# One two-bank PSUM tile kept for attention scores, single banks for every other matmul product

## The chip, the cores and the metric

The kernel runs on one core of a Trainium2 chip. The metric is the device time of one execution in microseconds (us). The kernel before took 1350.54 us (median of 3 runs, 1347.71 to 1353.4).

The core has five instruction streams that matter here: PE (the matrix engine, with its weight loads listed apart as PEld), DVE (vector), ACT (scalar), POOL (GpSimd) and SP, which issues the DMAs. Matmul results land in PSUM, which has 8 banks; one bank holds a 128 x 512 float32 block.

## The reference, cut to what matters

Two layers of a hybrid encoder over 512 tokens of width 1024. In each layer:

```python
h = rmsnorm(x)
proj = h @ w_in                      # group A: 8 q heads, 2 kv heads; group B: 4 heads with 2 q/k halves
# q and k: per-head RMSNorm, then rotary
ya = windowed_gqa_sink(qa, ka, va, sink)     # query blocks of 128, three neighbouring key blocks, mask
yb = diff_attention(qb, kb, vb, lam)         # softmax(first half) - lam * softmax(second half), all 512 keys
x = x + concat(ya, rmsnorm(yb)) @ w_out
h = rmsnorm(x)
gate, val = split(h @ w_up)                  # D_FF = 2816 = 22 blocks of 128
x = x + (silu(conv3(gate)) * val) @ w_down
```

Everything is float32. The kernel splits each operand into a high and a low part and forms each product from three matmuls (high x high, high x low, low x high), in `mm3` (L205).

## The kernel before

The residual stream `x` lies transposed in SBUF as 8 tiles of 128 x 512. Weights stream in as units of up to 512 KB. Each is copied to a high part by ACT (`wh`, L193) and its low part is formed by DVE or POOL (`wl`, L194); three such pairs of buffers exist, and `next_unit` prepares units up to three ahead.

A layer runs in these stages. `project` (L323) makes one 256-column chunk of the input projection for four token blocks, 24 matmuls a block; the first chunk is `akv`, then `aq0` and `aq1`, all run one after the other. Then `weave` (L133) interleaves two tracks by their written costs: `attend()` (L593), and a chain of the group-B projections (`proj_b`, L630) and the output projection (`out_pass`, `out_tail`). In `attend`, group A has 8 steps of `a_scores` and `a_values`, group B 16 steps of `b_scores`, `b_weights` and, for every second one, `b_values`. After the weave `out_last(1)` closes the output projection, the norm's factor `rb` is made (L686 to L692), and the feed-forward part (FFN) runs as two rounds: up-projection blocks `f` (12, then 10), then eight down-projection blocks `d`.

For each FFN block `f` there are two up products, gate and value, of 24 matmuls each. DVE multiplies the gate by `rb` (`gp`, L709), ACT, DVE and POOL do the convolution and the SiLU, DVE multiplies by the value product (L717), and `split_out` (L257) writes the result `act`. For each `d` a down product of 36 or 30 matmuls is added to `x` by DVE (L731).

PSUM before: tag `mm`, two single banks; tag `at`, two tiles of two banks each (`at2`, L94); `acc` and `tq`, one bank each. That is all eight banks.

- Scores take a two-bank `at` tile: `a_scores` two in turn for each step (L421), `b_scores` one for each step (L511).
- The transposed probabilities of group A, `pt`, take for key block 0 a two-bank `at` tile of which one half is used, for block 1 the `tq` bank, for block 2 an `mm` bank (L466). Those of group B, `wt`, take half of an `at` tile, and for the last head an `mm` bank (L540).
- `tq` also serves the transposes of q and k in `qk_out` (L366) and the two small products of `b_norm`. `mm` also serves `proj_b` and the output projection.
- `halves(both)` hands out the two halves of an `at` tile as two successive products (L390, L400). `halves(wide2)` does so for `out_last(1)` and the down products, and `wide2` for the two up products of a block: two times an `at` tile, every third time two `mm` banks.

The names in the profile show which it was: `up` and `dn` are halves of an `at` tile, `up_6a` or `dn_4b` is an `mm` bank.

The framework (Tile) assigns buffers and semaphores and orders the instructions of each engine when the kernel is built; on the chip each engine runs its list in that order.

Of the kernel before, what the change touches and what calls it, by code (L numbers as in the profile page):

```python
# [42 lines left out]
def kernel(  # L43
# [47 lines left out]
    def mm(name):  # L91
        return ps.tile([P, S], F32, tag="mm", bufs=2, name=name)

    def at2(name):  # L94
        return ps.tile([P, 2, S], F32, tag="at", bufs=2, name=name)

    def accum(name):
        return ps.tile([P, S], F32, tag="acc", bufs=1, name=name)
# [1 line left out]
    def tq(name):  # L100
        return ps.tile([P, S], F32, tag="tq", bufs=1, name=name)

    cyc = {"i": 0}

    def wide2(name):
        cyc["i"] += 1
        if cyc["i"] % 3 == 0:
            return mm(f"{name}a"), mm(f"{name}b")
        t = at2(name)
        return t[:, 0], t[:, 1]  # L110

    def halves(pick):
        have = []

        def alloc(name):
            if not have:
                have.extend(pick(name))
            return have.pop(0)
        return alloc

    def both(name):
        t = at2(name)
        return t[:, 0], t[:, 1]

    def run(gen):
        for _ in gen:
            pass
# [151 lines left out]
    for l in range(depth):  # L279
# [107 lines left out]
            split_out(va[0][:, t * P:(t + 1) * P], va[1][:, t * P:(t + 1) * P], raw[:, P:])  # L387
            qk_out(raw[:, :P], t, P, tabs[1], ka, "ka", None)

        run(project("akv", akv_done, halves(both)))  # L390
        rqa = sb.tile([P, NT, 4, 2], F32, tag="rqa", bufs=1, name=f"rqa{l}")
        rqb = sb.tile([P, NT, 4, 2], F32, tag="rqb", bufs=1, name=f"rqb{l}")
        qa = [(pair(f"qah{l}_{i}"), pair(f"qal{l}_{i}")) for i in range(2)]
# [3 lines left out]
                bank, t, CW, tabs[0], qa[i], f"qa{i}", rqa[:, t, 2 * i:2 * i + 2, :].rearrange("p a b -> p (a b)")), alloc)  # L397

        qk = {}
        pairs_at = halves(both)  # L400
        banks = iter((mm, mm, pairs_at, pairs_at, pairs_at, pairs_at, mm, mm))
        run(proj_a(0, lambda name: next(banks)(name)))
        run(proj_a(1, lambda name: next(banks)(name)))

        y_hi = [None] * 8
        y_lo = [None] * 8
# [5 lines left out]
        def a_scores(ip, qb):  # L412
            kb0, kb1 = max(qb - 1, 0), min(qb + 2, NT)
            n = (kb1 - kb0) * P
            m0 = (kb0 - qb + 1) * P
            nm = f"a{l}_{ip}_{qb}"
            q, k = qa[ip], ka
            mx = small(f"mx_{nm}", 4)
            so = []
            for i in range(2):  # L420
                sc = both(f"sc_{nm}_{i}")  # L421
                for j, (u, v) in enumerate(((0, 0), (0, 1), (1, 0))):
                    for g in range(2):
                        rs = slice(g * HD, (g + 1) * HD)
                        nc.tensor.matmul(sc[g][:, :n], lhsT=q[u][rs, i, qb * P:(qb + 1) * P],
                                         rhs=k[v][rs, kb0 * P:kb1 * P], start=j == 0, stop=j == 2)
                for g in range(2):
                    s = tmp(f"so_{nm}_{i}_{g}")
                    nc.vector.tensor_tensor_reduce(out=s[:, :n], in0=sc[g][:, :n], in1=mask_sb[:, m0:m0 + n],  # L429
                                                   op0=ALU.add, op1=ALU.max, scale=1.0, scalar=-3.0e38,  # L430
                                                   accum_out=mx[:, 2 * i + g:2 * i + g + 1])
                    so.append(s)
                yield 1.0
            by_g = lambda v: v.rearrange("p (g i) -> p i g", g=2)[:, 2 * ip:2 * ip + 2, :]
            pairs = lambda v: v.rearrange("p (i g) -> p i g", g=2)
            rq = rqa[:, qb, 2 * ip:2 * ip + 2, :]
            ngm = small(f"ng_{nm}", 4)
            nc.vector.tensor_tensor(out=pairs(mx), in0=pairs(mx), in1=rq, op=ALU.mult)
            nc.vector.scalar_tensor_tensor(out=pairs(ngm), in0=pairs(mx), scalar=-1.0, in1=by_g(nsink),
                                           op0=ALU.mult, op1=ALU.min)  # L440
            dn = small(f"dn_{nm}", 4)
            nc.vector.tensor_tensor(out=pairs(dn), in0=pairs(ngm), in1=by_g(sink), op=ALU.add)
            es = small(f"es_{nm}", 4)
# [12 lines left out]
            a_so[ip, qb] = so  # L456

        def a_values(ip, qb):
# [4 lines left out]
            pv = accum(f"pv_{nm}")  # L463
            pb = []
            for b in range(nkb):
                tr = mm(f"pt_{nm}_{b}") if b == 2 else both(f"pt_{nm}_{b}")[0] if b == 0 else tq(f"pt_{nm}_{b}")  # L466
                for g in range(2):
                    for i in range(2):
                        o = (2 * g + i) * P
                        nc.tensor.transpose(tr[:, o:o + P], so[2 * i + g][:, b * P:(b + 1) * P], ident)  # L470
                pt = prob(f"p_{nm}_{b}")
                split_out(pt[:, 0], pt[:, 1], tr)
                pb.append((pt[:, 0], pt[:, 1]))
                yield 0.5
# [25 lines left out]
        def b_scores(half, qb, j):  # L500
# [7 lines left out]
            rq = rqb[:, qb, h, :]  # L508
            q, k = qk[half]
            e = []  # L510
            sc2 = at2(f"sc_{nm}")  # L511
            sc = (sc2[:, 0], sc2[:, 1])
            for i, (u, v) in enumerate(((0, 0), (0, 1), (1, 0))):
                for c in range(2):
                    rs = slice(c * HD, (c + 1) * HD)
                    nc.tensor.matmul(sc[c], lhsT=q[u][rs, j, qb * P:(qb + 1) * P], rhs=k[v][rs, j, :],  # L516
                                     start=i == 0, stop=i == 2)
            nc.vector.tensor_reduce(out=mx, in_=sc2, axis=AX, op=ALU.max)
            nc.vector.scalar_tensor_tensor(out=mx, in0=mx, scalar=-1.0, in1=rq, op0=ALU.mult, op1=ALU.mult)  # L519
            for c in range(2):  # L520
                e.append(tmp(f"e_{nm}_{c}"))
# [11 lines left out]
        def b_weights(half, qb, j):  # L533
# [3 lines left out]
                b_st[half, j, "w"] = [prob(f"w{n}_b{l}_{h}_{qb}").rearrange("p a (b q) -> p (a b) q", b=2)  # L537
                                      for n in "hl"]
            wt = b_st[half, j, "w"]
            tr = (mm(f"wt_b{l}_{h}_{qb}") if half and j else both(f"wt_b{l}_{h}_{qb}")[0])  # L540
            for b in range(NT):
                nc.tensor.transpose(tr[:, b * P:(b + 1) * P], w[:, b * P:(b + 1) * P], ident)  # L542
            o = slice(qb % 2 * P, qb % 2 * P + P)
# [132 lines left out]
        def out_tail():  # L676
# [3 lines left out]

        weave((attend(), ATT),
              (chain(proj_b(0), proj_b(1), out_pass(0, mm), out_pass(1, mm), out_tail()), 98.6))
        run(out_last(1, w_last, halves(wide2)))
        norm.square(NK - 2)
        norm.square(NK - 1)
        r_tok2 = norm.rms()  # L686
# [11 lines left out]
        for pi, (f0, f1) in enumerate(FF_PARTS):  # L698
            act = []
            for f in range(f0, f1):  # L700
                acc = wide2(f"up{l}_{f}")
                for j in range(2):
                    w = next_unit()
                    for k in range(NK):
                        mm3(acc[j], (w[0][:, k, :], w[1][:, k, :]), (h.hi[k], h.lo[k]), k == 0, k == NK - 1)
                g = tmp(f"gp{l}_{f}", S + 2)
                nc.gpsimd.memset(g[:, 0:1], 0.0)
                nc.gpsimd.memset(g[:, S + 1:S + 2], 0.0)
# [10 lines left out]
                split_out(a[:, 0], a[:, 1], cv)  # L719
                act.append((a[:, 0], a[:, 1]))  # L720
            last = pi == len(FF_PARTS) - 1
            wide = halves(wide2)
            for d in range(NK):
                acc = wide(f"dn{l}_{pi}_{d}")
                nk = f1 - f0
# [85 lines left out]
```

## Time and profile before

| what | value |
|---|---|
| profiled execution, its own time | 1350.17 us |
| its span, first to last instruction | 1348.4 us |
| mean granted TensorE clock | 0.967 |
| runs | 1347.71, 1350.54, 1353.4 us |
| busy: DVE / ACT / POOL | 759.9 / 550.7 / 382.9 us |
| first layer: projections, attention, output projection | about 0 to 315 us |
| first layer: FFN | about 315 to 690 us |
| second layer: the same two parts | about 690 to 975 us, 975 to 1348 us |

How to read the lines below. A row of grouped instructions has line, engine, operation, what is written and read, shape and count, then busy time and the mean of one in ns, then the idle time of the engine just before them and what ended it. A row of waits has the waiting engine and line, what it waited for, and then total us, times, longest. A row of the timeline has start and duration in us; an idle time of the engine before the instruction stands in square brackets with what ended it. PE's matmuls are pipelined, so a matmul of 512 columns is listed with about 0.39 us while the next one starts about 0.23 us after it. A row of the chain of waits has start, length and the work that the end of the program hung on at that moment. A row of the windows has, for each engine, busy us and number of instructions in that stretch, then the granted clock.

### The profile page before, as it was taken

Reading aid. Unit: us, or ns where it says so; the run is one execution under the profiler, and the core shown is the slowest. Engines: PE = TensorE matmul, PEld = TensorE weight load, DVE = VectorE, ACT = ScalarE, POOL = GpSimd, SP = SyncE. Lnnn points to the kernel's source line nnn. Section 1 sums busy time; section 2 is a strip of 40 time slices with the busy share of each in tenths; the row PEclk is TensorE's granted clock in tenths of the full one; section 3 lists DMA queues with packets and bytes.
Section 4 is the critical chain, followed back from the end, with each engine's and each line's share of the span. In section 5 each row is a group of like instructions: output and inputs, shape, how many; then the busy total and the mean of one; then the engine's idle time right before and its main releaser. Section 6 shows DMA issues by size and latency. Waiting matters only on the chain.

```text
span 1348.4 us, 17285 instructions
## 1 busy us (share of the span) xinstructions
PE 1256.2 (93%) x6648; PEld 1048.1 (78%) x6648; DVE 759.9 (56%) x1345; ACT 550.7 (41%) x1003; POOL 382.9 (28%) x438
## 2 busy tenths in 40 slices
PE   6988799899999999999999688989999999999998
PEld 5977687687888778887788576967888887788876
DVE  6657687667555324554357676757755543355432
ACT  4445565445433212333345455634544331233321
POOL 5855377123211000110147461742221110011100
PEclk7998899699999999999999989989999999999999
DMA  4211122012332233332322020111133222333232
GB/s 167 82 44 32 40 63 63 16 47 79 95 101 90 82 101 94 98 100 69 98 91 63 32 63 8 57 63 32 48 99 104 94 87 90 106 94 97 83 102 78
DMA packets 32625, 102.93 MB, mean 76 GB/s; under 512 B 3616, under 2 KB 4000, under 8 KB 32544
## 3 DMA queue, kind: packets, MB, share of 16 engines
q1 hardware_dynamic: 32544, 101.84, 24.3%
q8 instruction: 52, 0.85, 0.3%
q14 instruction: 29, 0.24, 0.1%
HBM read 99.73 MB, written 2.10 MB: 76 GB/s over the span
## 4 chain that ended last, share of the span: by engine, by line
PE 75%; DVE 12%; ACT 5%; issue 4%; POOL 3%; DMA 1%; SPq 0%; POOLq 0%; ACTq 0%; DVEq 0%
PE up L207 8%; PE up L208 8%; PE up L206 8%; PE dn L207 4%; PE dn L206 4%; PE dn L208 4%; ACT so_a L447 2%; DVE so_a L454 2%; PE wo L206 1%; PE wo L207 1%; PE wo L208 1%; PE sc_b L516 1%; DVE so_a L429 1%; ACT wh L193 1%; PE wt_b L542 1%
## 5 line engine op out<-in xcount | busy, mean ns | idle before, releaser
L193 ACT CAST wh<-wr 128x1024 fp32r<-128x1024 f32 (+3 forms) x210 | 197.6, 945 | 401.4 <-PE up L207 151.7
L194 DVE TENSOR_TENSOR wl<-wr,wh 128x1024 fp32r<-128x1024 f32 (+3 forms) x174 | 191.7, 1105 | 170.0 <-ACT wh L193 165.0
L716 POOL TENSOR_TENSOR cv<-cv,rb 128x512 f32<-128x512 f32 x44 | 57.0, 1297 | 536.5 <-ACT cv L715 536.5
L207 PE MATMUL up<-nf_l,wh 128*128 128x512 f32 x464 | 180.9, 390 | 1.0 <-DVE nf_l L225 1.0
L206 PE MATMUL up<-nf_h,wh 128*128 128x512 f32 x464 | 180.6, 389 | 0.0
L208 PE MATMUL up<-nf_h,wl 128*128 128x512 f32 x464 | 180.5, 389 | 0.0
L194 POOL TENSOR_TENSOR wl<-wr,wh 128x1024 fp32r<-128x1024 f32 x36 | 86.7, 2413 | 99.4 <-ACT wh L193 85.7
L207 PEld LDWEIGHTS up<-nf_l,wh 128*128 128x128 f32 x464 | 87.1, 188 | 19.7 <-DVE nf_l L225 1.9
L206 PE MATMUL dn<-act,wh 128*128 128x512 f32 x240 | 96.1, 400 | 6.4 <-ACT wh L193 3.5
L206 PEld LDWEIGHTS up<-nf_h,wh 128*128 128x128 f32 x464 | 87.1, 188 | 18.1
L208 PEld LDWEIGHTS up<-nf_h,wl 128*128 128x128 f32 x464 | 87.1, 188 | 17.8
L207 PE MATMUL dn<-act,wh 128*128 128x512 f32 x240 | 95.9, 400 | 0.4 <-DVE act L259 0.4
L208 PE MATMUL dn<-act,wl 128*128 128x512 f32 x240 | 94.9, 398 | 0.0
L522 ACT ACTIVATE e_b<-sc_b,mx_b,rqb 128x512 f32<-128x512 f32 x64 | 49.3, 775 | 49.0 <-DVE mx_b L519 42.2
L709 DVE TENSOR_TENSOR gp<-up,rb 128x512 f32<-128x512 f32 x29 | 20.1, 692 | 80.6 <-PE up L208 79.6
L206 PEld LDWEIGHTS dn<-act,wh 128*128 128x128 f32 x240 | 45.4, 189 | 20.9 <-ACT wh L193 4.3
L715 ACT ACTIVATE cv<-cv 128x512 f32<-128x512 f32 x44 | 27.6, 632 | 79.7 <-DVE cv L714 79.6
L207 PEld LDWEIGHTS dn<-act,wh 128*128 128x128 f32 x240 | 45.8, 191 | 11.9 <-DVE act L259 1.1
L208 PEld LDWEIGHTS dn<-act,wl 128*128 128x128 f32 x240 | 45.4, 189 | 10.6
L206 PE MATMUL pj_bv<-wh,na_h 128*128 128x256 f32 x128 | 41.0, 320 | 7.7 <-DVE vb L376 7.7
L731 DVE TENSOR_TENSOR x<-x,dn 128x512 f32<-128x512 f32 x22 | 15.1, 688 | 52.8 <-PE dn L208 52.8
L470 PE MATMUL pt_a<-ident,so_a 128*128 128x128 f32 x160 | 28.3, 293 | 17.3 <-DVE so_a L454 12.0
(506 smaller groups left out, 3268.6 us busy)
## 6 DMA issues: line engine op xcount, KB each, us to landing
wr<-w_up SPq DMA_DIRECT2D x88, 512.0 KB, 3.6
wr<-w_in SPq DMA_DIRECT2D x36, 512.0 KB, 3.5
wr<-w_down SPq DMA_DIRECT2D x32, 384.0 KB, 3.1
wr<-w_down SPq DMA_DIRECT2D x32, 320.0 KB, 2.9
wr<-w_out SPq DMA_DIRECT2D x16, 512.0 KB, 3.7
x<-xT SPq DMA_DIRECT2D x8, 256.0 KB, 5.7
outT<-x SPq DMA_DIRECT2D x8, 256.0 KB, 2.0
rows<-row_par SPq DMA_DIRECT2D x2, 260.0 KB, 4.2
```

The costliest lines, as they stand in the source:

```text
L193: nc.scalar.copy(hi[:, o], raw[:, o])
L194: eng.tensor_tensor(out=lo[:, o], in0=raw[:, o], in1=hi[:, o], op=ALU.subtract)
L206: nc.tensor.matmul(acc, lhsT=a[0], rhs=b[0], start=start, stop=False)
L207: nc.tensor.matmul(acc, lhsT=a[0], rhs=b[1], start=False, stop=False)
L208: nc.tensor.matmul(acc, lhsT=a[1], rhs=b[0], start=False, stop=stop)
L447: nc.scalar.activation(so[i][:, :n], so[i][:, :n], AF.Exp, bias=ngm[:, i:i + 1], scale=rqa[:, qb, 2 * ip + i // 2, i % 2:i % 2 + 1], accum ...
L454: nc.vector.tensor_scalar(out=so[i][:, :n], in0=so[i][:, :n], scalar1=rl[:, i:i + 1], scalar2=None, op0=ALU.mult)
L470: nc.tensor.transpose(tr[:, o:o + P], so[2 * i + g][:, b * P:(b + 1) * P], ident)
L522: nc.scalar.activation(e[c], sc[c], AF.Exp, bias=mx[:, c:c + 1], scale=rq[:, c:c + 1], accum_out=lsum[:, c:c + 1])
L709: nc.vector.tensor_tensor(out=g[:, 1:S + 1], in0=acc[0], in1=rb, op=ALU.mult)
L715: nc.scalar.activation(cv, cv, AF.Silu)
L716: nc.gpsimd.tensor_tensor(out=cv, in0=cv, in1=rb, op=ALU.mult)
```

## The change

Tag `at` becomes two single banks, and a new tag `sc` holds one two-bank tile. PSUM is again full: `mm` 2, `at` 2, `sc` 2, `acc` 1, `tq` 1.

- Scores of both groups take the one `sc` tile.
- `pt` takes the two `at` banks in turn, for all key blocks; `wt` takes an `at` bank, and as before an `mm` bank for the last head.
- `akv`, `aq0`, `aq1` take `mm` and `at` banks in turn (`turn`).
- `out_last(1)`, the up products and the down products take `mm`, `at`, `mm`, `at` and one half of `sc` in a round of five (`wide`). Each up product now has a tile of its own.

No instruction is added or removed; what changes is where products land, and with it buffers, waits and the order that the framework makes.

```diff
-    def at2(name):
-        return ps.tile([P, 2, S], F32, tag="at", bufs=2, name=name)
+    def at(name):
+        return ps.tile([P, S], F32, tag="at", bufs=2, name=name)
+
+    def sc2(name):
+        return ps.tile([P, 2, S], F32, tag="sc", bufs=1, name=name)
...
-    def wide2(name):
+    def wide(name):
         cyc["i"] += 1
-        if cyc["i"] % 3 == 0:
-            return mm(f"{name}a"), mm(f"{name}b")
-        t = at2(name)
-        return t[:, 0], t[:, 1]
-
-    def halves(pick):
...
-    def both(name):
-        t = at2(name)
-        return t[:, 0], t[:, 1]
+        i = cyc["i"] % 5
+        return sc2(name)[:, 0] if i == 4 else (mm, at)[i % 2](name)
+
+    def turn(name):
+        cyc["i"] += 1
+        return (mm, at)[cyc["i"] % 2](name)
...
-        run(project("akv", akv_done, halves(both)))
+        run(project("akv", akv_done, turn))
...
-        pairs_at = halves(both)
-        banks = iter((mm, mm, pairs_at, pairs_at, pairs_at, pairs_at, mm, mm))
-        run(proj_a(0, lambda name: next(banks)(name)))
-        run(proj_a(1, lambda name: next(banks)(name)))
+        run(proj_a(0, turn))
+        run(proj_a(1, turn))
...
-                sc = both(f"sc_{nm}_{i}")
+                scp = sc2(f"sc_{nm}_{i}")
+                sc = (scp[:, 0], scp[:, 1])
...
-                tr = mm(f"pt_{nm}_{b}") if b == 2 else both(f"pt_{nm}_{b}")[0] if b == 0 else tq(f"pt_{nm}_{b}")
+                tr = at(f"pt_{nm}_{b}")
...
-            sc2 = at2(f"sc_{nm}")
-            sc = (sc2[:, 0], sc2[:, 1])
+            scp = sc2(f"sc_{nm}")
+            sc = (scp[:, 0], scp[:, 1])
...
-            tr = (mm(f"wt_b{l}_{h}_{qb}") if half and j else both(f"wt_b{l}_{h}_{qb}")[0])
+            tr = (mm if half and j else at)(f"wt_b{l}_{h}_{qb}")
...
-        run(out_last(1, w_last, halves(wide2)))
+        run(out_last(1, w_last, wide))
...
             for f in range(f0, f1):
-                acc = wide2(f"up{l}_{f}")
+                acc = []
                 for j in range(2):
                     w = next_unit()
+                    a = wide(f"up{l}_{f}_{j}")
                     for k in range(NK):
-                        mm3(acc[j], (w[0][:, k, :], w[1][:, k, :]), (h.hi[k], h.lo[k]), k == 0, k == NK - 1)
+                        mm3(a, (w[0][:, k, :], w[1][:, k, :]), (h.hi[k], h.lo[k]), k == 0, k == NK - 1)
+                    acc.append(a)
...
-            wide = halves(wide2)
             for d in range(NK):
                 acc = wide(f"dn{l}_{pi}_{d}")
```

More of the change, by code (lines that the diff above doesn't have):

```diff
@@ L103 @@
     cyc = {"i": 0}
-    def wide2(name):
+    def wide(name):
         cyc["i"] += 1
-        if cyc["i"] % 3 == 0:
-            return mm(f"{name}a"), mm(f"{name}b")
-        t = at2(name)
-        return t[:, 0], t[:, 1]
-    def halves(pick):
[L113 to L119, printed above, removed]
-    def both(name):
-        t = at2(name)
-        return t[:, 0], t[:, 1]
+        i = cyc["i"] % 5
[3 more added lines that the diff above has]
+        return (mm, at)[cyc["i"] % 2](name)
     def run(gen):
@@ L517, in b_scores @@
                                      start=i == 0, stop=i == 2)
-            nc.vector.tensor_reduce(out=mx, in_=sc2, axis=AX, op=ALU.max)
+            nc.vector.tensor_reduce(out=mx, in_=scp, axis=AX, op=ALU.max)
             nc.vector.scalar_tensor_tensor(out=mx, in0=mx, scalar=-1.0, in1=rq, op0=ALU.mult, op1=ALU.mult)
```

## The prediction

> **What bounds the kernel now.** I read the page first, then the windows by stage, then the chain of waits and PE's own waits in the stages that have gaps.
>
> ```profile
> span 1348.4 us, 17285 instructions
> PE 1256.2 (93%) x6648; PEld 1048.1 (78%) x6648; DVE 759.9 (56%) x1345; ACT 550.7 (41%) x1003; POOL 382.9 (28%) x438
> PE 75%; DVE 12%; ACT 5%; issue 4%; POOL 3%; DMA 1%; SPq 0%; POOLq 0%; ACTq 0%; DVEq 0%
> ```
>
> PE is busy for 93% of the span, and three quarters of the chain that ends last is PE. The rest is PE waiting. Where it waits, the windows tell (us of the stretch, then busy us and count of PE, PEld, DVE, ACT, POOL, then the granted clock):
>
> ```profile
> 60.00:180.00 120.00, 100.35 (x685) 86.67 (x684) 83.80 (x228) 64.21 (x165) 59.63 (x57) 0.91 0.15 47
> 235.00:300.00 65.00, 56.99 (x306) 45.39 (x307) 41.75 (x77) 27.84 (x56) 10.62 (x6) 0.84 0.10 30
> 315.00:443.00 128.00, 128.00 (x572) 106.22 (x573) 69.03 (x82) 47.07 (x59) 20.54 (x41) 1.00 0.31 95
> 443.00:507.00 64.00, 61.51 (x260) 48.30 (x259) 22.72 (x27) 14.83 (x18) 1.37 (x3) 1.00 0.30 91
> ```
>
> In the up-projection (315 to 443) PE never stops. In the down-projection (443 to 507) it does, with every other engine under half busy. In group A's attention (60 to 180) and in the end of group B's (235 to 300) it stops more, and the granted clock falls to 0.91 and 0.84. The change touches all four places in a different way, so I cost them apart.
>
> **Down products: the wait inside a shared tile.** Chain of waits near the end of the first layer (start, length, what):
>
> ```profile
> 674.41 0.02 issue
> 674.43 0.70 DVE x L731
> 675.26 0.47 PE dn L206
> ```
>
> One down product ends, DVE adds it to `x`, and only then does PE begin the next. The two are the halves of one `at` tile, in different banks: the framework keeps the second half's first matmul behind the read of the first half. Where it can, it slips a later product in:
>
> ```profile
> 645.00 0.39 PE L208 MATMUL dn<-act,wl 128*128 128x512 f32 x1
> 646.02 0.50 PE L206 MATMUL dn_4a<-act,wh 128*128 128x512 f32 x1 [0.63 <-ACT wh L193]
> ```
>
> Here the halves were those of `d` 2 and 3. PE turned to `d` 4, whose weights were not copied yet, so the wait is named ACT, but its origin is the same. All waits of this kind (total us, times, longest):
>
> ```profile
> PE dn L206 <- ACT wh L193: 3.5, 5, 0.9
> PE dn_2a L206 <- ACT wh L193: 1.4, 2, 0.7
> PE dn L206 <- DVE x L731: 1.7, 2, 0.9
> PE dn_6a L206 <- ACT wh L193: 0.7, 1, 0.7
> PE dn_4a L206 <- ACT wh L193: 0.6, 1, 0.6
> ```
>
> That is 11 waits, 7.9 us. The rotation of `wide2` gives 16 pairs of down products, of which 5 lie in `mm` (`dn_2a`, `dn_4a`, `dn_0a`, `dn_6a` and once more `dn_2a`) and 11 in `at`: one wait for each `at` pair and none for an `mm` pair. A listed idle time begins at the modelled end of a matmul, 0.39 us after its start, while matmuls otherwise follow at 0.23, so each wait loses 0.16 more: 7.9 + 11 x 0.16 = 9.7 us. With single banks each pair becomes like `mm`'s, and nothing of this lies beside other PE work. What is late next: the weights of the next `d`, which the `mm` pairs have in time. I take all 9.7; the bounds are 1.7 + 2 x 0.16 = 2.0 (only the waits named DVE) and 9.7.
>
> **Up products: the gate waits for its value.** DVE's timeline:
>
> ```profile
> 1027.40 0.69 DVE L709 TENSOR_TENSOR gp<-up,rb 128x512 f32<-128x512 f32 x1 [3.31 <-PE up L208]
> 1038.28 0.69 DVE L709 TENSOR_TENSOR gp<-up,rb 128x512 f32<-128x512 f32 x1 [2.71 <-PE up L208]
> 1043.72 0.69 DVE L709 TENSOR_TENSOR gp<-up_6a,rb 128x512 f32<-128x512 f32 x1 [1.86 <-PE up_6a L208]
> ```
>
> Two blocks in `at` are 10.88 us apart, two products of 5.44; the block after them, in `mm`, has its gate only 5.44 later. So an `at` gate waits until the value product too is done. That costs nothing while PE has more up products, but at the end of a round the down products need the last `act`. Second layer, second round, chain of waits and then PE's timeline:
>
> ```profile
> 1287.82 0.70 DVE cv L717
> 1288.54 0.63 ACT act L258
> 1289.19 0.70 DVE act L259
> 1292.51 0.43 PE dn L206
> ...
> 1289.21 0.50 PE L206 MATMUL dn<-act,wh 128*128 128x512 f32 x1 [1.19 <-ACT act L258]
> 1289.93 0.50 PE L207 MATMUL dn<-act,wh 128*128 128x512 f32 x1 [0.23 <-DVE act L259]
> ```
>
> The two waits lose 1.19 + 0.23 + 2 x 0.16 = 1.7 us, and afterwards some 8 matmuls run at 0.43 instead of 0.23, another 1.6 (the row at 1292.51 is one of them). With the gate 5.44 us earlier, `act` is ready about that much earlier, or at worst 2.0 us (0.70 + 0.63 + 0.70) after the last value product; both are in time. Gain 3.3, between 0 (if ACT's weight copies then stand in the way) and 3.3. The FFN together: 9.7 + 3.3 = 13.0 us.
>
> **FFN, five banks for six.** In steady state a bank comes round after 5 x 5.44 = 27 us and is held for its 5.44 and the few us until DVE has read it; down products are longer still. The tight place is the head of the second layer's FFN, where `rb` comes late and nothing is released meanwhile:
>
> ```profile
> 1004.42 0.69 DVE L717 TENSOR_TENSOR cv<-cv,up_0b 128x512 f32<-128x512 f32 x1 [2.09 <-POOL cv L716]
> 1005.44 0.39 PE L206 MATMUL up_3a<-nf_h,wh 128*128 128x512 f32 x1
> ```
>
> The seventh product begins at 1005.44. In a round of five it takes the second one's bank, free at 1005.11. Slack 0.3 us: I take 0, bounds 0 and 2 (a `rb` two us later, in one layer).
> The Trainium skill's page "Perfetto Trace Analysis", section "Matmul Optimizations", wants all eight PSUM banks in use, and here six in rotation become five. By that rule the FFN would slow down; the rows above have room for it in one place only.
>
> **Attention, what goes.** Scores, `pt`, `wt`, q/k transposes and projections no longer share banks, but for the last head. PE's waits for another product's bank:
>
> ```profile
> PE pt_a L470 <- DVE bql L259: 5.3, 2, 3.8
> PE sc_b L516 <- DVE p_a L259: 2.2, 2, 1.9
> PE sc_b L516 <- DVE wl_b L259: 1.2, 3, 0.6
> PE sc_a L425 <- DVE p_a L259: 1.1, 1, 1.1
> ```
>
> Together 9.8 us over both layers (the first is `pt` behind a q transpose in `tq`). PE works in a fixed order, so a wait that goes may uncover one for data just behind it; I take 6, bounds 0 and 9.8, the lower where every wait has another behind it.
>
> **Attention, what comes.** One score tile in place of two. The lengths, by groups and from the chain of waits, and last the window of the tail for `sc_b` alone (DVE's 8 maxima are 8 steps):
>
> ```profile
> L429 DVE CUSTOM_DVE_ANT_0 so_a<-sc_a,mask_sb 128x384 f32<-128x384 f32 x32 | 16.1, 552 | 7.6 <-PE pt_a L470 7.6
> L518 DVE TENSOR_REDUCE mx_b<-sc_b 128x2 f32<-128x1024 f32 x32 | 38.9, 1216 | 4.6 <-PE sc_b L516 4.6
> L259 DVE TENSOR_TENSOR p_a<-pt_a,p_a 128x512 fp32r<-128x512 f32 x40 | 26.7, 683 | 0.5 <-ACT p_a L258 0.2
> L258 ACT CAST p_a<-pt_a 128x512 fp32r<-128x512 f32 x40 | 22.4, 584 | 23.1 <-PE pt_a L470 22.9
> ...
> 122.45 0.73 PE sc_a L425 x6
> 183.21 0.89 PE sc_b L516 x6
> 239.22 1.64 ACT e_b L522 x4
> ...
> 235.00:300.00 65.00, 10.16 (x48) 5.14 (x48) 9.74 (x8) 13.03 (x32) 0.84 0.10 30
> ```
>
> Group A: the second tile's six matmuls (0.73) now wait for both masked maxima of the first (2 x 0.55), and DVE for them: at most 16 steps x 0.73 = 11.7. Queued behind PE's wait are projections, `pv` products and transposes, and ACT's exponentials wait for the maxima. But a step takes 120 / 8 = 15 us and its two scores in a row 2 x (0.73 + 1.10) = 3.7, so the order has room: I take 4. Third `pt` block: two `at` banks for three blocks, so it waits for the first block's copy and difference, 0.58 + 0.68 = 1.27, in the 40 - 2 x 16 = 8 steps that have three: at most 10.2; I take 2, since PE has projections to go on with. Group B: the next scores wait for the exponentials (1.64) instead of running beside them, at most 0.89 for each of the 32 steps, 28; but a step alone takes 0.89 + 1.22 + 1.64 = 3.75 against 65 / 8 = 8.1 us in the tail and `proj_b` fills PE before it, so only steps that follow closely pay: I take 3. Behind that wait stand `wt` transposes and output products, and L518 waits for the scores. Sum 9, bounds 0 (a wait more gains nothing by itself) and 50; I stay near the low end because PE's row 60 to 180 has work of its own for 100 of 120 us.
>
> `akv`, `aq0`, `aq1` over single banks: no price, PE is held by the matmuls themselves. No DMA moves, and no queue is passed.
>
> **Sum.** Against the profiled execution's 1350.2 (span 1348.4 and 1.8 around it, 0.4 under the median): 1350.2 - 13.0 - 6 + 9 = 1340.2, so 1340.
>
> **Rivals.** Single scores decide (slower): in both groups the score chain becomes the longest one, each of the 16 A steps pays 0.73, each third block 1.27, and the 16 steps of the two tails 0.89 and half as much again at a lower clock: 11.7 + 10.2 + 21 = 43, less 6 and 13: 1374 at full price. From 26 us of attention cost on it is slower by over 0.5%. For it: the chain of waits runs through L447, L454 and L518 where PE has gaps. Against it: 3.7 of 15 us.
> The page "TensorE: Matmul & The Clock Gate", section "Part 1: The HAM clock gate", has the clock halve after an idle window of about 3.4 us, and by it a tail with more waits would lose more than their sum. The rows agree in part: 0.84 in the tail, and 0.43 for 0.23 after 1289.93, though no single wait there was that long.
>
> Attention gains too: the removed bank waits come back whole and the new ones hide: 1350.2 - 13.0 - 9.8 = 1327, or some us less if the clock of 0.91 recovers. For it: in the 120 us of A no engine but PE is over 70% busy.
>
> Nearly no change: either the waits named ACT are truly late weights, and only 2.0 of the 9.7 goes (1350.2 - 2.0 - 3.3 + 3 = 1348), or attention loses about what the FFN gains.
>
> Five banks are too few: `rb` is later in the new order and the FFN's head stalls in both layers, 2 each: 1344, at the border of the same.
>
> **Numbers.** Forecast 0.42 (1332 to 1344), attention gains too 0.20, nearly no change 0.18, five banks 0.05, scores decide 0.15. 0.5% is 6.7 us, about what a measurement of this kernel can tell: faster means below 1343.8. Faster 0.42 + 0.20 = 0.62, same 0.18 + 0.05 = 0.23, slower 0.15. The range takes in 1327 with a little clock, and goes up past the same: 1322 to 1358.
>
> **What would show it.** Right: no wait of a `dn` product for ACT `wh` or DVE `x` in the middle of a down-projection, about 3 us less in each of the first layer's two; `gp` 5.44 us apart throughout; no wait of `pt` for `bql`. Wrong: `dn` waits that stay; waits of `sc_a` for L429 or of `sc_b` for L522 that sum to over 10 us; a stretch from 60 to 300 that has grown by more than 10.

## The result, and the profile after

The changed kernel takes 1303.74 us (median of 4 runs, 1300.81 to 1304.01), beside 1350.68 for the kernel before on the same chip: ratio 0.9648, 95% interval 0.9623 to 0.9673, faster. A second set of 5 runs gave 1302.88 us, 0.9635 (0.9616 to 0.9655). The forecast was 1340 with a range of 1322 to 1358, so the result lies 18 us below the range. The profiled execution took 1303.46 us.

The page of the kernel after, its span and busy times:

```profile
span 1301.2 us, 17328 instructions
PE 1242.6 (95%) x6648; PEld 1040.4 (80%) x6648; DVE 763.8 (59%) x1345; ACT 551.7 (42%) x1003; POOL 383.7 (29%) x438
```

The engines do the same work: the counts of all five are those of the kernel before, and the 43 instructions that the first row has more are of kinds that are not counted as busy. The span is 47.2 us shorter. In the new numbering a line is 7 to 9 lower: `mm3` is L198 to L200, `split_out` L250 and L251, the scores L416 and L507, `pt` L461, the gate `gp` L702.

Four stages divide the span but for some 4 us at its end, each measured between the starts of its first and last matmuls (us; the two layers with a slash):

| stage | before | after | difference |
|---|---|---|---|
| start, or last `dn`, to first `sc_a` (projections `akv`, `aq`) | 60.6 / 37.9 | 55.6 / 36.6 | -6.2 |
| first `sc_a` to last `wo` (attention, output projection) | 249.2 / 250.4 | 236.5 / 236.9 | -26.2 |
| last `wo` to first `dn`, and the up products of the second round | 242.73 / 241.97 | 242.45 / 242.45 | +0.2 |
| four rounds of down products | 261.01 | 246.55 | -14.5 |

The down rounds first, by the windows (stretch, then PE, PEld, DVE, ACT, POOL busy with counts, granted clock, DMA). The kernel before, its four rounds:

```profile
443.48:514.20 70.72, 68.23 (x288) 53.74 (x287) 24.16 (x28) 15.88 (x19) 1.37 (x3) 1.00 0.31 92
623.30:682.10 58.80, 56.67 (x240) 44.74 (x239) 24.76 (x32) 21.51 (x31) 9.06 (x7) 1.00 0.32 94
1103.40:1172.50 69.10, 67.71 (x289) 53.87 (x288) 24.01 (x28) 15.87 (x19) 1.37 (x3) 1.00 0.32 94
1281.50:1343.80 62.30, 58.80 (x241) 45.87 (x239) 19.31 (x26) 12.18 (x17) 1.34 (x1) 0.97 0.30 93
```

The kernel after:

```profile
425.50:492.80 67.30, 67.30 (x289) 54.10 (x288) 21.61 (x25) 14.43 (x17) 0.11 (x3) 1.00 0.33 96
601.80:657.80 56.00, 56.00 (x240) 45.02 (x239) 24.72 (x32) 21.55 (x31) 8.35 (x7) 1.00 0.34 99
1064.80:1132.10 67.30, 67.30 (x289) 54.10 (x288) 21.61 (x25) 14.41 (x17) 0.08 (x3) 1.00 0.33 96
1241.10:1297.10 56.00, 56.00 (x241) 45.01 (x239) 17.08 (x23) 10.83 (x15) 0.03 (x1) 1.00 0.33 104
```

PE is now busy for the whole of each stretch, and the list of PE's waits has none for a `dn` or `up` product. The end of the second layer's second round, DVE's timeline after:

```profile
1235.84 0.69 DVE L702 TENSOR_TENSOR gp<-up,rb 128x512 f32<-128x512 f32 x1 [3.09 <-PE up L200]
...
1241.35 0.69 DVE L710 TENSOR_TENSOR cv<-cv,up 128x512 f32<-128x512 f32 x1 [2.33 <-PE up L200]
```

The last gate is read 5.5 us before the last value product, one product earlier than a shared tile allowed. PE goes from the last up product (1240.86) to the first down product (1241.08) without a wait.

Attention with the output projection, first layer, by the windows, before and then after:

```profile
60.60:309.80 249.20, 220.00 (x1426) 187.32 (x1426) 177.66 (x402) 129.32 (x298) 117.05 (x109) 0.92 0.15 46
```
```profile
55.60:292.10 236.50, 215.75 (x1424) 182.61 (x1424) 169.96 (x401) 126.05 (x293) 116.00 (x108) 0.94 0.15 46
```

Nearly the same matmuls, 29.2 us of idle PE before and 20.8 after, at a higher clock. Group A alone, in the first layer after (its counterpart, 60 to 180, stood at a clock of 0.91):

```profile
55.00:160.00 105.00, 97.33 (x714) 85.61 (x715) 79.57 (x227) 64.37 (x166) 59.26 (x58) 0.98 0.18 54
```

PE's longest waits after (what it waited for, total us, times, longest):

```profile
PE sc_b L507 <- ACT e_b L513: 10.7, 8, 3.3
PE wt_b L533 <- DVE e_b L521: 8.6, 5, 3.4
...
PE tr_bk L361 <- DVE bkl L251: 4.9, 3, 2.7
PE pj_bq L198 <- ACT raw_bq L335: 4.0, 2, 2.0
PE pt_a L461 <- DVE so_a L445: 3.1, 2, 2.2
PE sc_a L416 <- DVE mx_a L420: 2.8, 5, 1.1
```

The single score tile does cost something: group B's scores now wait 10.7 us for the exponentials of the step before. It is outweighed. No wait of `pt` for `bql` is left, and nothing in this list is as large as the gain. In both layers together idle PE in this stage fell from 62.4 to 42.6 us, and PE was busy for 430.8 us with the same matmuls in place of 437.2.

### The profile page after: what moved, and what is told of

It reads as the page before. It is cut to its first block, busy times and chain, and to the rows that moved or that the text cites. A ratio compares the mean times of both kernels' runs of the same rounds, so it can differ in the third digit from the quotient of the medians.

```text
span 1301.2 us, 17328 instructions
## 1 busy us (share of the span) xinstructions
PE 1242.6 (95%) x6648; PEld 1040.4 (80%) x6648; DVE 763.8 (59%) x1345; ACT 551.7 (42%) x1003; POOL 383.7 (29%) x438
## 5 line engine op out<-in xcount | busy, mean ns | idle before, releaser
L199 PE MATMUL up<-nf_l,wh 128*128 128x512 f32 x704 | 274.9, 391 | 0.3
L198 PE MATMUL up<-nf_h,wh 128*128 128x512 f32 x704 | 274.0, 390 | 0.0
L200 PE MATMUL up<-nf_h,wl 128*128 128x512 f32 x704 | 273.5, 390 | 0.5
L199 PEld LDWEIGHTS up<-nf_l,wh 128*128 128x128 f32 x704 | 132.1, 188 | 30.4 <-DVE nf_l L217 3.5
L200 PEld LDWEIGHTS up<-nf_h,wl 128*128 128x128 f32 x704 | 132.2, 188 | 28.9 <-DVE wl L186 2.0
L198 PEld LDWEIGHTS up<-nf_h,wh 128*128 128x128 f32 x704 | 132.1, 188 | 27.6 <-ACT nf_h L216 0.5
L200 PE MATMUL dn<-act,wl 128*128 128x512 f32 x352 | 139.5, 397 | 0.0
L199 PE MATMUL dn<-act,wh 128*128 128x512 f32 x352 | 139.4, 397 | 0.0
L198 PE MATMUL dn<-act,wh 128*128 128x512 f32 x352 | 138.8, 395 | 0.0
L702 DVE TENSOR_TENSOR gp<-up,rb 128x512 f32<-128x512 f32 x44 | 30.3, 692 | 101.4 <-PE up L200 96.3
L199 PEld LDWEIGHTS dn<-act,wh 128*128 128x128 f32 x352 | 66.8, 190 | 16.5
L198 PEld LDWEIGHTS dn<-act,wh 128*128 128x128 f32 x352 | 66.0, 188 | 16.5
L200 PEld LDWEIGHTS dn<-act,wl 128*128 128x128 f32 x352 | 66.1, 188 | 15.5
L509 DVE TENSOR_REDUCE mx_b<-sc_b 128x2 f32<-128x1024 f32 x32 | 39.0, 1220 | 10.8 <-PE sc_b L507 10.6
```

What stands on the lines that cost most here:

```text
L198: nc.tensor.matmul(acc, lhsT=a[0], rhs=b[0], start=start, stop=False)
L199: nc.tensor.matmul(acc, lhsT=a[0], rhs=b[1], start=False, stop=False)
L200: nc.tensor.matmul(acc, lhsT=a[1], rhs=b[0], start=False, stop=stop)
L509: nc.vector.tensor_reduce(out=mx, in_=scp, axis=AX, op=ALU.max)
L702: nc.vector.tensor_tensor(out=g[:, 1:S + 1], in0=acc[0], in1=rb, op=ALU.mult)
```

## The experiments

The theory on trial first was that the attention gain comes from one part, the place of `pt`. The rivals were the scores' own tile, the single banks of the projections, and an effect of the new order that no bank explains. Each table row gives the median time, the ratio to the kernel before with its 95% interval, the length of attention with output projection in each layer (as in the table above), and the sum of the four down rounds. The kernel before was run beside every group, with medians of 1350.5 to 1353.7, so kernels of different groups are compared by ratio.

| kernel | us | ratio | attention | down |
|---|---|---|---|---|
| before | 1350.68 | 1 | 249.2 / 250.4 | 261.0 |
| after | 1303.74 | 0.9648 (0.9623 to 0.9673) | 236.5 / 236.9 | 246.6 |
| before, FFN in single banks | 1338.87 | 0.9897 (0.9875 to 0.9919) | 249.1 / 252.5 | 246.6 |
| before, projections in single banks | 1347.45 | 0.9974 (0.9959 to 0.9989) | 257.0 / 250.0 | 261.1 |
| before, scores in a tile of their own | 1349.01 | 0.9969 (0.9954 to 0.9985) | 250.8 / 246.0 | 261.1 |
| before, all `pt` in `at` | 1322.33 | 0.9771 (0.9745 to 0.9797) | 239.9 / 234.0 | 259.5 |
| after, `pt` in `at`, `tq`, `mm` | 1334.69 | 0.9861 (0.9844 to 0.9877) | 257.2 / 249.4 | 246.6 |
| after, `pt` block 1 in `tq` | 1312.23 | 0.9688 (0.9661 to 0.9715) | 248.6 / 236.2 | 246.6 |
| after, `pt` block 2 in `mm` | 1309.82 | 0.9673 (0.9649 to 0.9696) | 243.2 / 239.7 | 246.6 |
| after, `pt` in `mm`, `tq`, `at` | 1340.67 | 0.9920 (0.9898 to 0.9942) | 257.0 / 256.9 | 246.6 |

**FFN in single banks, alone.** The kernel before with `mm` and one half of an `at` tile in turn (`turn`) for each up and down product: four banks in rotation, not five.

```diff
-                acc = wide2(f"up{l}_{f}")
+                acc = []
                 for j in range(2):
                     w = next_unit()
+                    acc.append(turn(f"up{l}_{f}_{j}"))
...
-            wide = halves(wide2)
+            wide = turn
```

> The kernel before, with only the up and down products of the FFN put one to a tile (a round of four: the two mm banks and the first half of each at tile). If the framework's wait inside a shared two-bank tile made the gaps of the FFN, the four down rounds are 14.5 us shorter together, as they are in the changed kernel, the attention is as before, and the time is 1350.7 - 14.5 = 1336. If the weights' copies made them, the dn waits stay and the time is 1348 or more. If fewer banks in rotation cost the FFN, four must cost more than five: over 1340.

The down rounds are those of the kernel after, 67.3, 56.0, 67.3 and 56.0, and attention is about as before. The ratio is worth 13.9 us of 1350.7. So the FFN's share comes from tiles that are not shared. Four banks show as too few in one place, the one that the prediction named for five: at the head of the second layer's FFN an up product waits for a gate:

```profile
PE up L211 <- DVE gp L715: 2.0, 1, 2.0
```

That stage (last `wo` to first `dn`) takes 136.7 us in place of 132.9; with five it takes 133.4. Not all of the 3.8 us need be the banks' doing: in the first layer the stage takes 131.5 in place of 133.7, and in the kernel before with another order (weave cost 84, below) the two take 137.8 and 130.2.

**Projections alone.** The kernel before with `akv`, `aq0` and `aq1` over `mm` and `at` in turn.

```diff
-        run(project("akv", akv_done, halves(both)))
+        run(project("akv", akv_done, turn))
...
-        run(proj_a(0, lambda name: next(banks)(name)))
-        run(proj_a(1, lambda name: next(banks)(name)))
+        run(proj_a(0, turn))
+        run(proj_a(1, turn))
```

> The kernel before, with only akv, aq0 and aq1 put one product to a tile (mm and the first half of an at tile in turn). The stretch up to the first scores of both layers was 6.2 us shorter in the changed kernel. If that is the projections' own doing: 6 us less, 1344.5, and group A as before. If an earlier and smoother start of the projections is also what shortened group A: 1320 to 1330. If neither: 1350.

The first `sc_a` comes at 53.9 in place of 60.6, 6.7 us earlier, and the attention of the first layer then takes 257.0 in place of 249.2. The stage's gain is real and is given back behind it: 0.9974, some 3.5 us.

**Scores alone.** The kernel before with the scores in a two-bank tile `sc` of their own and one `at` tile for `pt` block 0 and `wt`. The pairs of products of the projections and of the FFN take the two tiles in turn (not in the cut).

```diff
-                sc = both(f"sc_{nm}_{i}")
+                sc = sboth(f"sc_{nm}_{i}")
...
-            sc2 = at2(f"sc_{nm}")
+            sc2 = scp(f"sc_{nm}")
```

> The kernel before, with only the scores taken out of the shared at tag: they get a two-bank tile of their own, and pt block 0, wt and all pairs of products share the other one. Theory 'scores' (group A lost its 27.6 us because scores and transposed probabilities queued for the same two tiles): most of it comes back, 1323 to 1332. Theory 'pt' (it lost them because pt's three blocks lay in three tags shared with others): little, 1346 to 1352, or slower because score tiles are single now.

Its waits of PE, the first two groups of scores:

```profile
PE sc_b L529 <- ACT e_b L535: 12.7, 8, 3.2
PE sc_a L438 <- DVE mx_a L442: 10.0, 8, 2.3
```

These are the waits that the prediction priced, 22.7 us of them, and still the kernel is not slower: 0.9969. Others shrank at the same time: `pt` for `so_a` from 12.0 to 4.8, and `tr_bk` for `bkl` (8.1), `pj_bv` for `vb` (7.7) and `pt` for `bql` (5.3) are gone, although `pt` still has its places in `tq` and `mm`. Idle PE in the attention stages is 55.0 us in place of 62.4; the projections before them take 4.4 us longer. Named waits do not add up to time here.

**The place of `pt`, both ways.** The kernel before with every `pt` block in one half of an `at` tile, and the kernel after with the blocks back in `at`, `tq` and `mm`.

```diff
-                tr = mm(f"pt_{nm}_{b}") if b == 2 else both(f"pt_{nm}_{b}")[0] if b == 0 else tq(f"pt_{nm}_{b}")
+                tr = both(f"pt_{nm}_{b}")[0]
```
```diff
-                tr = at(f"pt_{nm}_{b}")
+                tr = (at, tq, mm)[b](f"pt_{nm}_{b}")
```

> The kernel before with only pt changed: all blocks in at tiles (half of each), none in tq or mm, while scores still share these two tiles. If leaving tq and mm is what counts: 1350.7 - 31 = 1320, with group A about 13 us shorter in each layer. If pt must also be free of the scores: at most 10 us less, 1341 or more.

> The changed kernel with only pt put back to three tags: block 0 in an at bank, block 1 in tq, block 2 in an mm bank. Theory 'pt': group A gets most of its 27.6 us back, about 1325 to 1331. Theory 'scores': stays within 3 us of 1304. If only tq matters, somewhere between, with waits of pt_a for bql or of tr_bk for p_a back in the list.

This is the main term. One line moves the kernel before by 2.3%, 31 us, although its `pt` blocks then share two tiles with the scores, and the same line moves the kernel after by 29 us (0.9861 - 0.9648 = 0.0213) the other way. With it alone the attention stages of the kernel before take 474.0 us together, against 499.6 before and 473.4 after the whole change. Windows of the first layer's attention, the kernel before with `pt` in `at`, then the kernel after with `pt` in the old places:

```profile
59.70:299.60 239.90, 216.82 (x1425) 181.72 (x1425) 171.80 (x402) 128.71 (x298) 118.23 (x109) 0.95 0.16 48
```
```profile
53.70:311.00 257.30, 223.39 (x1424) 188.27 (x1424) 169.14 (x402) 125.56 (x293) 116.30 (x109) 0.91 0.14 43
```

Idle PE is 23.1 us in the first and 33.9 in the second, the clock 0.95 and 0.91. PE's waits in the second kernel have hardly one of `pt` for the other track's bank (the last row):

```profile
PE sc_b L507 <- ACT e_b L513: 13.1, 9, 3.2
PE sc_a L416 <- DVE mx_a L420: 11.4, 7, 3.2
...
PE pv_a L198 <- ACT p_a L250: 5.9, 6, 1.9
PE pv_a L198 <- DVE yl L251: 5.6, 3, 2.6
PE pt_a L461 <- DVE so_a L445: 4.0, 6, 1.8
...
PE pt_a L461 <- DVE bkl L251: 0.3, 1, 0.3
```

The first two are waits for the one score tile (10.7 and 2.8 us in the kernel after), and `pv` for `yl` is one for the `acc` bank of the step before (1.9 after). `pv` for `p_a` (0.2 after) and `pt` for `so_a` (3.1 after) are waits for data. So the price of the shared tags stands here under other names. The order in which the framework wrote PE's list shows how `pv` comes to wait for `p_a`. The first step of group A in the kernel after, from its last `pt` transposes to its first `pv` product (left out between them: 31 projection matmuls, the scores and a pair of q transposes):

```profile
72.86 0.49 PE L461 MATMUL pt_a<-ident,so_a 128*128 128x128 f32 x3
...
78.00 0.39 PE L198 MATMUL pv_a<-p_a,va 128*128 128x512 f32 x1
```

The same place in the kernel with the old `pt` (left out: two projection matmuls):

```profile
74.18 0.27 PE L461 MATMUL pt_a<-ident,so_a 128*128 128x128 f32 x1
74.21 0.36 PE L200 MATMUL pj_bv<-wh,na_l 128*128 128x256 f32 x1
...
74.64 0.28 PE L200 MATMUL pj_bv<-wh,na_l 128*128 128x256 f32 x1
74.86 0.62 PE L416 MATMUL sc_a<-ka,qah 64*128 64x384 f32 x4
75.31 0.34 PE L416 MATMUL sc_a<-ka,qal 64*128 64x384 f32 x2
75.58 0.44 PE L361 MATMUL tr_qa<-ident,raw_qa 128*128 128x128 f32 x2
77.57 0.49 PE L198 MATMUL pv_a<-p_a,va 128*128 128x512 f32 x1 [1.55 <-ACT p_a L250]
```

In the kernel after, both `pt` blocks are transposed together and `pv` stands behind some 5 us of projections, so `p_a` is there when PE comes to it. With the second block in `tq`, the tag of the q/k transposes, only the first block is transposed at this point, and `pv` is written four projections, six score matmuls and one pair of q transposes later: PE stands for 1.55 us. That the framework writes `pv` there because `tq` is taken was not tried by itself. It is one part of the price: over both layers' attention idle PE is 64.1 us against 42.6 in the kernel after, and the same matmuls keep PE busy for 442.6 us against 430.8, at a lower clock.

**One tag at a time.** The kernel after with only block 1 in `tq`, and with only block 2 in `mm`.

> The changed kernel with only pt block 1 put back to the tq bank (blocks 0 and 2 stay in at). 'tq' theory (the one bank that the q and k transposes of qk_out also need held group A): most of the 31 us that pt in three tags cost returns, 1325 to 1335. 'mm' theory (block 2 between the projections' products): stays at 1302 to 1310. Both half: about 1318.

> The changed kernel with only pt block 2 put back to an mm bank (blocks 0 and 1 stay in at). 'mm' theory: 1325 to 1335. 'tq' theory: 1302 to 1310, or a little less than the changed kernel, since three blocks then have three banks.

0.9688 and 0.9673 beside 0.9648: about 5 and 3 us, with intervals that overlap that of the kernel after (7 and 5 us beside its second set, 0.9635). Both tags together cost 0.9861 - 0.9648 = 0.0213, 29 us. The costs of the two tags do not add.

**Two score tiles in the tail.** To see whether the new waits of `sc_b` can be had back: in group B's second half every other step's scores go to the two `at` banks (two maxima of 512 in place of one of 1024), and its `wt` to `mm`.

```diff
-            scp = sc2(f"sc_{nm}")
-            sc = (scp[:, 0], scp[:, 1])
+            b_n["i"] += 1
+            own = half and b_n["i"] % 2
+            scp = None if own else sc2(f"sc_{nm}")
+            sc = [at(f"sc_{nm}_{c}") for c in range(2)] if own else (scp[:, 0], scp[:, 1])
```

> The changed kernel with a second place for scores in the second half of group B: every other step puts its two score products into the two at banks (two maxima of 512 in place of one of 1024), and wt goes to an mm bank for that half. If the single score tile holds the tails (waits of sc_b for e_b, 10.7 us in all): 1303.7 less 6 to 12, 1292 to 1298. If the tails wait for the softmax chain whatever the banks: 1302 to 1306. If wt in mm now queues with the output products: slower, 1306 to 1312.

It gave 1300.15 us, 0.9601 (0.9578 to 0.9624). Because that lay so near the kernel after, both were run again on one chip:

> The changed kernel once more, beside the next one on the same chip: 0.965 of the kernel before, 1303 to 1306.

> The changed kernel with every other score tile of group B's second half in the two at banks, once more. If its 3.6 us are real: 0.960 of the kernel before and below the changed kernel by 2 to 5 us. If they were chance: the same as the changed kernel within 2.

1302.88 us, 0.9635 (0.9616 to 0.9655), and 1301.97 us, 0.9630 (0.9611 to 0.9650): no difference that can be measured. PE's waits of that version in the second set of runs:

```profile
PE tr_bk L361 <- DVE bkl L251: 7.6, 4, 2.9
...
PE yb L198 <- ACT wh_b L250: 4.7, 6, 1.3
...
PE wt_b L540 <- ACT e_b L520: 3.4, 2, 1.7
...
PE sc_b L510 <- ACT e_b L520: 2.6, 2, 2.4
```

The wait of `sc_b` falls from 10.7 to 2.6 us, and others grow, that of `tr_bk` from 4.9 to 7.6 and that of `yb` from 1.5 to 4.7. The wait for the score tile is one that another stands behind.

**Sharing, or one unlucky order?** The same three shared tags in another assignment, and the kernel before with nothing but the weave's cost of attention changed.

```diff
-                tr = at(f"pt_{nm}_{b}")
+                tr = (mm, tq, at)[b](f"pt_{nm}_{b}")
```
```diff
-ATT = 92.0
+ATT = 105.0
```

> The changed kernel, with the pt blocks in the three tags of the kernel before in another assignment: block 0 in mm, block 1 in tq, block 2 in at. Theory 'sharing' (pt in the tags that the projections and the q/k transposes hold at the same time makes the cost, whichever block it is): the same tags are shared, so 1325 to 1340, group A of either layer back near 118 us from its first scores to its last pt. Theory 'one order' (the 31 us belong to the one order that the framework happened to write for that kernel): another order, so anywhere, most likely 1304 to 1318, where the two kernels that shared a single tag were.

> The kernel before with one number changed, the written cost of the attention track in the weave, 92 to 105, so that attention steps are put earlier among the projections; no bank and no instruction changes. Theory 'order' (a good part of the attention time hangs on the order that is written at build time, not on who waits for which bank): the time moves by 10 us or more either way, through waits of PE for data in group A. Theory 'banks' (the bank waits are the cost): the banks are the same, so within 7 us of the kernel before.

The swapped tags gave 1340.67 us, 38 us above the kernel after in the same group (1302.88): shared tags cost no less in another assignment. But the weave's cost alone, with the same banks, made the kernel before slower too: 1372.61 us, 1.0155 (1.0135 to 1.0175). PE's waits there, four of the largest, of `pt` and the q/k transposes:

```profile
PE tr_qa L369 <- DVE qal L259: 10.7, 4, 4.3
PE pt_a L470 <- DVE bkl L259: 8.1, 2, 4.2
PE tr_bk L369 <- DVE bkl L259: 7.4, 7, 1.7
...
PE pt_a L470 <- DVE vb L376: 5.9, 2, 3.2
```

`pt` for `bkl` (in `tq`) and for `vb` (in `mm`) are waits for the other track's bank, 14.0 us. In this order the sharing shows under its own name. So neither theory had it alone, and the two were set against each other: the kernel after with its own `pt` banks and with the shared ones, each at two further weave costs, with `ATT = 105.0` or `ATT = 84.0`.

> The changed kernel with the weave's cost of attention 105 in place of 92. Theory 'sharing': pt has banks of its own, so an attention step that comes earlier costs little: 1300 to 1318, and the kernel with shared tags at the same cost is 25 or more above it. Theory 'order': this moves as the kernel before did, by +22, to about 1325, or anywhere.

> The changed kernel with weave cost 105 and the pt blocks in at, tq, mm as before the change. Theory 'sharing': 25 to 45 above the kernel with own tags at 105; the price shows as waits of pt for tq's and mm's users or as waits of scores and pv for data. Theory 'order': within 12 of it, or below it.

> The changed kernel with weave cost 84: attention steps later among the projections. Theory 'sharing': 1300 to 1318. Theory 'order': anywhere.

> The changed kernel with weave cost 84 and the pt blocks in at, tq, mm. Theory 'sharing': 15 to 45 above the kernel with own tags at 84 (less than at 105, since pt comes later and finds its banks free more often). Theory 'order': within 12 of it, or below it.

| weave cost | own banks | shared banks | difference |
|---|---|---|---|
| 84 | 1303.58, 0.9650 (0.9620 to 0.9680) | 1328.29, 0.9829 (0.9804 to 0.9853) | 24.7 us |
| 92 | 1303.74, 0.9648 (0.9623 to 0.9673) | 1334.69, 0.9861 (0.9844 to 0.9877) | 29 us, by the ratios |
| 105 | 1342.61, 0.9933 (0.9912 to 0.9955) | 1346.31, 0.9956 (0.9939 to 0.9972) | 3.7 us, intervals overlap |

In two orders of three, sharing costs 25 to 29 us, as the theory of sharing has it. In the third it costs next to nothing, although `pt` waits 7.4 us for its bank in `tq` there (for `bkl` 5.6, for `qal` 1.8), and the kernel with its own banks is itself 39 us slower, from the order alone. The largest wait of that kernel is for the score tile, 8.6 us more than at cost 92:

```profile
PE sc_b L507 <- ACT e_b L513: 19.3, 10, 5.3
PE pv_a L199 <- DVE p_a L251: 6.7, 3, 3.3
```

That is a part of it. Its attention stages take 42.8 us longer than at cost 92: idle PE is 22.0 us more, and the same matmuls keep PE busy for 20.8 us more, at a clock of 0.90 and 0.89 in the two layers in place of 0.94.

**The kernel before in the better order.** Its weave cost was then taken the other way, to 84.

> The kernel before with weave cost 84, no bank changed. If the measured gain of the change is in part a better order that the kernel before could have had as well: 1320 to 1340, and the change is worth less than 47 us. If the banks carry it: 1345 to 1360, with the waits of pt and of the q/k transposes for each other's banks still there.

1340.29 us, 0.9917 (0.9900 to 0.9934): 11 us of what the change brought were to be had from the order, without touching a bank. Against this version the change at the same cost is worth 0.9917 - 0.9650 = 0.0267, 36 us.

## Why the prediction was right in one half and wrong in the other

Beside the profiled execution the forecast is 36.7 us too high (1340.2 less 1303.5). Attention makes 29.2 of this: -6 and +9 were forecast, and the stages became 26.2 us shorter. The projections make 6.2, where nothing was forecast, and the FFN 1.3 (14.3 for 13.0).

- **Down and up products: right.** The step "9.7 + 3.3 = 13.0 us" measured 14.5 (the four down rounds), and 13.9 as a kernel by itself. The waits named ACT `wh` were indeed the tile's, since all 11 are gone. "`gp` 5.44 us apart throughout" was badly put: consecutive gates are two products apart in either kernel, and what moved is the gate against its own value product, by one product.
- **Five banks for six: right.** From the last `wo` to the first `dn` the first layer takes 0.3 us less and the second 0.5 more, within the bounds of 0 and 2. The rule of the Trainium skill that was weighed there ("Perfetto Trace Analysis", section "Matmul Optimizations": all eight banks in use) begins to show with four banks in rotation, as one wait of 2.0 us in the second layer and none in the first.
- **`akv`, `aq0`, `aq1`, "no price": wrong**, by 6.2 us in the stage itself (6.7 in the first layer with that part alone). The step took PE to be held by the matmuls. Yet in the first layer's stage PE stood idle for 13.4 us before and 11.4 after, and the clock was 0.89 and 0.94. Alone, most of it was given back in attention.
- **Attention, "what goes": the step that failed.** It gave "I take 6, bounds 0 and 9.8", the upper bound being the sum of four entries of PE's list. The place of `pt` alone was worth 31 us in the kernel before. Three things were missing in the bound. First, it counted waits of scores and `pt` only. The same list has waits of the other products for a bank of `tq` or `mm` (L259, L376 and L655 read that bank):

```profile
PE tr_bk L369 <- DVE bkl L259: 8.1, 6, 2.5
PE pj_bv L206 <- DVE vb L376: 7.7, 4, 2.7
...
PE wo L206 <- DVE x L655: 2.7, 1, 2.7
```

  With all `pt` in `at` they are 3.9, 2.5 and none; with the whole change 4.9, 0.2 and none. With the four entries they make 28.3 us, of which 8.5 are left with all `pt` in `at`, beside 2.6 of a new kind (`pt` for a score's tile). That is 17.2 us less; idle PE in the attention stages fell by 20.6, from 62.4 to 41.8. (Most of these waits are gone as well in the kernel with the scores' change alone, which leaves `pt` where it was, so the order decides on them too.) Second, matmuls that run are part of the price: those stages kept PE busy for 437.2 us before and 432.2 with all `pt` in `at`, at a clock of 0.92 and 0.95 in the first layer. Third, a shared bank need not show under its name: with the old places in the kernel after most of the price showed as waits for the score tile and for data, with another order in PE's list, and as a lower clock. The sum of one kind of wait was not an upper bound.

  In PE's waits of the kernel before, the longest entry of group A was one for data, also left out of that sum; it is 3.1 us after:

```profile
PE pt_a L470 <- DVE so_a L454: 12.0, 8, 2.0
```

  Four of these waits, 7.4 us, ended behind `so_a` steps of DVE of 2.5 us each, where the median of the 64 steps is 0.41. The long steps ran beside a `wl` of POOL; here four steps of `so_a`, two of them long:

```profile
80.44 5.60 DVE L454 TENSOR_SCALAR so_a<-so_a,rl_a 128x384 f32<-128x384 f32 x4
81.01 4.81 POOL L194 TENSOR_TENSOR wl<-wr,wh 128x1024 fp32r<-128x1024 f32 x2 [2.77 <-ACT wh L193]
```

  The kernel after has five `so_a` steps over 2.2 us as well, but PE waits little for them. So a part of the gain may come from where the order puts POOL's `wl`, and not from a bank; this was not tried by itself.

- **Attention, "what comes", +9:** the waits came about as priced or larger (`sc_b` for `e_b` 10.7, where 3 were taken; `sc_a` for the maxima 2.8, where 4 were taken), except that of the third `pt` block (none, where 2 were taken), but the kernel with the scores' change alone was 0.3% faster, not slower. With the reordering around it, this term has no size of its own. Waits of `sc_b` of over 10 us were named as a sign of being wrong; they came, and attention was shorter all the same.
- **The rivals.** "Attention gains too" had the direction right and stopped at 1327, or some us less by the clock, because it used the same bound. "Scores decide" did not come true in the order as shipped; at weave cost 105, where `sc_b` waits 19.3 us, it is part of what makes the kernel 39 us slower.
- **The clock.** PE's waits of the first layer's group A before, the one with the longest single wait:

```profile
PE pj_bv L206 <- DVE vb L376: 3.9, 2, 2.7
```

No wait there is longer than 2.7 us, and the granted clock stood at 0.91; with fewer waits it stands at 0.98. The Trainium skill's page "TensorE: Matmul & The Clock Gate", section "Part 1: The HAM clock gate", speaks of an idle window of about 3.4 us. The trace agrees that idleness lowers the clock, but here waits of half that length were enough. One case, in the kernel before: in a stretch of 3.4 us PE was busy for 1.61, its one wait there 1.82, and in the next stretch the granted clock is 0.50 (the third figure from the end of a row):

```profile
99.90:103.30 3.40, 1.61 (x15) 1.18 (x13) 1.69 (x9) 3.38 (x11) 1.08 (x2) 1.00 0.01 2
103.40:106.70 3.30, 3.30 (x16) 2.35 (x16) 3.24 (x11) 1.50 (x4) 0.00 (x0) 0.50 0.00 0
```

The parts taken alone, 0.0103 (FFN) + 0.0026 (projections) + 0.0031 (scores) + 0.0229 (`pt`) = 0.0389, stand against 0.0352 to 0.0365 for all together. What stays open: why the two shared tags cost 3 to 5 us each and 29 together, and why the price vanishes at weave cost 105. Both seem to lie in the order that the framework writes, which these runs show but do not change one step at a time.

## What to carry to other kernels

Where a framework writes the order of the engines when the kernel is built, a buffer shared between two interleaved tracks can cost more than the waits that carry its name. Add up those waits in both tracks, look at what stands between each producer and its consumer in PE's list, and price a change of buffers by trying it with two or three orders. Give every product that is read by itself a tile of its own, even if the rotation gets shorter: two products in one tile were worth 14 us here, and a rotation of five banks in place of six cost 0.2. Before crediting a change with its time, move the neighbouring tuning number in the kernel before as well: here 11 of the 47 us were there for the taking.

## What the runs showed that was not expected

- One written number, the weave's cost of attention, moved the kernel before from 0.9917 (84) over 1 (92) to 1.0155 (105), and the kernel after from 0.9650 over 0.9648 to 0.9933, with the same instructions and the same banks.
- Waits of 22.7 us for a single score tile came with no loss of time (0.9969): other waits shrank, and idle PE in attention was 55.0 us in place of 62.4.
- A wait of PE of 1.8 us was followed by over 3 us at half the clock.
